# A planner's order replaced by a written one in the first third of a transformer block

## The chip, the cores and the metric

The kernel runs on one core of one Trainium2 chip, as a single program. The metric is device time in microseconds (us) from start to end; lower is better. Engines are called as the profile calls them: PE (matrix unit), PEld (its weight loads), DVE (vector), ACT (activation), POOL (GpSimd), SP (the engine that issues most transfers).

## The reference, cut to what matters

One layer over 512 latent tokens and 256 context tokens, each 1024 wide, float32.

```
h   = rmsnorm(x)   * (1 + scale)   + shift        # scale, shift = silu(c)     @ w_ada + b_ada
hc  = rmsnorm(ctx) * (1 + scale_c) + shift_c      #                c_ctx in place of c
q_c (384) | kv_c (256) | k_rope (32) | gla q,k,v (512 each) | gla gate | decay inputs (2x16) | merge gates = h @ w_in
attention, 8 heads:  q = rope(rmsnorm(q_c) @ w_uq)     k, v = rmsnorm(kv_c of h and hc) @ w_ukv, plus rope(k_rope)
                     o = softmax(q k^T / sqrt(96)) v   # 512 queries, 768 keys
gated linear attention, 4 heads, both directions, on gla q,k,v with decays from w_decay
mix = (sigmoid gates * the two branches) @ w_out;  x = x + gate1 * mix
x = x + gate2 * (gelu(conv3x3(h2 @ w_up_gate)) * (h2 @ w_up)) @ w_down;   out = rmsnorm(x) * final_g
```

## The kernel before

All matrix products keep near-float32 accuracy by splitting each operand into a high part (a cast by ACT) and a low part (a subtraction by DVE or POOL), and summing three products on PE: `mm3` (lines 124 to 128) issues high*high (line 126), high*low (127) and low*high (128). `mm` (131) is one plain product. A helper that records for every caller has one line in the profile: `sub` is line 118, `tt` 115, the ACT cast in `split` 122.

The stages that the change touches all lie in the pool `e1`:

1. **Start.** Parameter rows, the constants and the token tiles `xs[t]` (128 tokens by 1024) are loaded, the tokens' squares summed on ACT (line 366), the tokens scaled on DVE (370), and silu of the two conditioning vectors is made.
2. **Column loop**, j = 0 to 7 over the 128-column blocks of the model width. `modulation(j)` multiplies the conditioning by two 512 KB blocks of `w_ada` (32 small matmuls), copies the result (400), and turns it into the per-column shift and scale `shc`, `scc` (403, 404). `modulated(j)` transposes the tokens' block j on PE (411), applies shift and scale on ACT (413) and makes the high (416) and low (118) parts. `latents(j)` accumulates two kv and three q blocks in PSUM over j; its weights come from `load_w(j)` (320 KB into a `kT` buffer), split by ACT and POOL. `in_turn` (328 to 335) chains these loads on SP's queue, in the order in which they are written. At j = 3 `decay_weights` also issues two loads and six copies between tiles (450) on SP.
3. **Norm chain.** Squares of the kv and q latents, their sums by a one-column matmul, the factor 1/rms on ACT and DVE (170 to 179), spread over partitions by PE, and the normalised kv latents. Context tokens have a chain of their own, and q a third. `misc` projects the rope key and the decay inputs. The up-projection of q takes 128 columns a head: 64 plain, 32 rope, and the 32 rope columns again with their pairs swapped, which DVE copies out of the split weights (599, twelve copies).
4. **Attention.** For each head: `softmax(h)` makes scores for four blocks of 128 queries (six matmuls each), their maximum on DVE (694), the exponential on ACT (696), a reciprocal on DVE (697) and the scaling on POOL (698). `prep_q` makes a head's queries, whose high and low parts are both made on DVE (612, 118). `attend(h)` does six steps: four transposes of the weights (726), a high cast on ACT (729), the low part on DVE (118, tile `pl`), four matmuls with the values. `heads_out` splits a head's result (708, 710).
5. **Values of the linear attention**, `gla_v(half, t)`: 6 token tiles by 2 halves of 256 columns, 24 matmuls each; some placed between attention steps, the rest behind. Gated linear attention, merge and feed-forward follow and are not changed.

The order on each engine isn't the order of the source. The kernel is built with a planner (`schedule_with_timeline_sim`), which places each instruction by its own estimate of when it can start; `tc.issue_after` fixes single pairs. Each engine then executes its list strictly in order, so an instruction that waits holds up all behind it on its engine.

## Time and profile before

| | |
|---|---|
| median of 3 runs | 924.19 us (923.54 to 924.62) |
| the profiled execution | 922.85 us, span 921.0 us, mean granted PE clock 0.997 |
| busy PE / DVE / ACT / POOL | 890.9 / 590.5 / 400.2 / 377.4 us |
| PE matmuls | 5008 |
| loaded from memory | 97.65 MB |

The span runs from the first to the last instruction. A matmul's recorded duration includes its way through the array, so that in a steady stream the records overlap; the pace is the distance of two starts, not the duration. PE can thus be shown as busy and still not be at its pace.

### The profile page before, as it was taken

Reading aid. Unit: us, or ns where it says so; the run is one execution under the profiler, and the core shown is the slowest. Engines: PE = TensorE matmul, PEld = TensorE weight load, DVE = VectorE, ACT = ScalarE, POOL = GpSimd, SP = SyncE. Lnnn points to the kernel's source line nnn. Section 1 sums busy time; section 2 is a strip of 40 time slices with the busy share of each in tenths; the row PEclk is TensorE's granted clock in tenths of the full one; section 3 lists DMA queues with packets and bytes.
Section 4 is the critical chain, followed back from the end, with each engine's and each line's share of the span. In section 5 each row is a group of like instructions: output and inputs, shape, how many; then the busy total and the mean of one; then the engine's idle time right before and its main releaser. Section 6 shows DMA issues by size and latency. Waiting matters only on the chain.

```text
span 921.0 us, 12993 instructions
## 1 busy us (share of the span) xinstructions
PE 890.9 (97%) x5008; PEld 757.2 (82%) x5008; DVE 590.5 (64%) x984; ACT 400.2 (43%) x661; POOL 377.4 (41%) x222
## 2 busy tenths in 40 slices
PE   4989999999999999999999999999999999999996
PEld 3768788889988888888888889888888888888885
DVE  3568987867667676775674584987787876400006
ACT  3455566774445454533545232443334243422105
POOL 3354132563243434243463522354444454376403
PEclk9999999999999999999999999999999999999998
DMA  9763000042231515143981611534343433244102
GB/s 318 247 170 104 0 2 1 1 138 89 61 103 35 149 35 145 40 125 102 314 277 63 183 46 51 155 93 135 115 139 92 137 92 109 76 153 144 46 1 91
DMA packets 131229, 100.77 MB, mean 109 GB/s; under 512 B 5754, under 2 KB 122722, under 8 KB 131168
## 3 DMA queue, kind: packets, MB, share of 16 engines
q1 hardware_dynamic: 130096, 97.56, 34.9%
q0 software_dynamic: 816, 2.09, 0.7%
q8 instruction: 39, 0.64, 0.3%
q10 hardware_dynamic: 256, 0.30, 0.1%
q14 instruction: 22, 0.18, 0.1%
HBM read 97.65 MB, written 2.10 MB: 108 GB/s over the span
## 4 chain that ended last, share of the span: by engine, by line
PE 84%; DVE 4%; ACT 1%; issue 0%; ACTq 0%; DVEq 0%
PE pb L126 18%; PE pb L127 18%; PE pb L128 18%; PE p L126 7%; PE p L128 7%; PE p L127 7%; PE pb L131 4%; PE p L131 3%; PE pb L726 2%; DVE s L118 1%; DVE kT L118 1%; DVE mx L694 1%; DVE s L115 0%; PE pb L1116 0%; ACT P L696 0%
## 5 line engine op out<-in xcount | busy, mean ns | idle before, releaser
L118 POOL TENSOR_TENSOR wlo<-raw,whi 128x1024 fp32r<-128x1024 f32 (+2 forms) x113 | 257.2, 2285 | 308.2 <-ACT whi L122 281.5
L126 PE MATMUL pb<-s,whi 128*128 128x512 f32 (+1 forms) x625 | 242.4, 388 | 0.0
L127 PE MATMUL pb<-s,whi 128*128 128x512 f32 (+1 forms) x625 | 240.6, 385 | 0.0
L128 PE MATMUL pb<-s,wlo 128*128 128x512 f32 (+1 forms) x625 | 240.3, 384 | 0.0
L122 ACT CAST whi<-raw 128x1024 fp32r<-128x1024 f32 (+1 forms) x108 | 106.4, 986 | 157.3 <-issue 65.2
L128 PEld LDWEIGHTS pb<-s,wlo 128*128 128x128 f32 x625 | 117.6, 188 | 23.2
L127 PEld LDWEIGHTS pb<-s,whi 128*128 128x128 f32 x625 | 117.7, 188 | 22.7 <-issue 0.7
L126 PEld LDWEIGHTS pb<-s,whi 128*128 128x128 f32 x625 | 117.7, 188 | 22.6
L1175 DVE SCALAR_TENSOR_TENSOR ac<-pb,cwT,ac 128x441 f32<-128x441 f32 (+2 forms) x160 | 110.9, 693 | 17.9 <-ACT ac L1166 14.0
L115 DVE TENSOR_TENSOR p<-p,gt 128x512 f32<-128x512 f32 x4 | 2.8, 700 | 98.5 <-PE p L128 98.4
L126 PE MATMUL pb<-whi,s 128*128 128x256 f32 (+1 forms) x168 | 55.2, 330 | 0.0
L127 PE MATMUL pb<-wlo,s 128*128 128x256 f32 (+1 forms) x168 | 55.1, 328 | 0.0
L128 PE MATMUL pb<-whi,s 128*128 128x256 f32 (+1 forms) x168 | 55.0, 328 | 0.0
L126 PE MATMUL p<-s,s 128*128 128x512 f32 (+1 forms) x130 | 48.3, 373 | 6.7 <-DVE s L416 4.8
L698 POOL TENSOR_SCALAR P<-P,rs 128x768 f32<-128x768 f32 x32 | 29.5, 925 | 53.0 <-DVE rs L697 51.0
L127 PE MATMUL p<-s,s 128*128 128x512 f32 (+1 forms) x130 | 47.6, 366 | 0.3 <-DVE s L118 0.3
L128 PE MATMUL p<-s,s 128*128 128x512 f32 (+1 forms) x130 | 47.6, 366 | 0.0
L1177 ACT ACTIVATE ac<-ac 128x512 f32<-128x512 f32 x22 | 13.9, 633 | 76.7 <-DVE ac L1175 76.7
L126 PE MATMUL p<-s,whi 128*128 128x256 f32 (+1 forms) x130 | 43.3, 333 | 0.0
L128 PE MATMUL p<-s,wlo 128*128 128x256 f32 (+1 forms) x130 | 43.1, 332 | 0.0
L127 PE MATMUL p<-s,whi 128*128 128x256 f32 (+1 forms) x130 | 42.8, 330 | 0.0
L118 DVE TENSOR_TENSOR pl<-pb,ph 128x512 fp32r<-128x512 f32 x48 | 32.3, 683 | 12.2 <-ACT ph L729 11.9
(284 smaller groups left out, 1763.5 us busy)
## 6 DMA issues: line engine op xcount, KB each, us to landing
raw<-in_w_up_dram SPq DMA_DIRECT2D x44, 512.0 KB, 3.7
raw<-in_w_in_dram SPq DMA_DIRECT2D x32, 512.0 KB, 3.8
s<-in_w_ada_dram SPq DMA_DIRECT2D x22, 512.0 KB, 5.7
raw<-in_w_down_dram SPq DMA_DIRECT2D x22, 512.0 KB, 3.3
raw<-in_w_ada_dram SPq DMA_DIRECT2D x16, 512.0 KB, 3.8
xn<-in_w_ada_dram SPq DMA_DIRECT2D x10, 512.0 KB, 4.1
kT<-in_w_in_dram SPq DMA_DIRECT2D x8, 320.0 KB, 5.3
s<-in_x_dram SPq DMA_DIRECT2D x4, 512.0 KB, 5.4
```

The source lines that it names most:

```text
L115: return eng.tensor_tensor(out=out_, in0=a, in1=b, op=op)
L118: eng.tensor_tensor(out=out_, in0=a, in1=b, op=ALU.subtract)
L122: A.copy(hi, src)
L126: PE.matmul(o, lhsT=sh, rhs=mh, start=first, stop=False)
L127: PE.matmul(o, lhsT=sh, rhs=ml, start=False, stop=False)
L128: return PE.matmul(o, lhsT=sl, rhs=mh, start=False, stop=last)
L131: PE.matmul(o, lhsT=a, rhs=b, start=first, stop=last)
L694: V.tensor_reduce(out=mx, in_=sp[:, 0:768], op=ALU.max, axis=AX.X, negate=True)
L698: G.tensor_scalar(out=pt, in0=pt, scalar1=rs, scalar2=1.0, op0=ALU.mult, op1=ALU.mult)
L726: PE.transpose(tp[:, m * 256 + n * 128:m * 256 + (n + 1) * 128], P[2 * half + n][:, (2 * kk + m) * 128:(2 * kk + m + 1) * 128], ident)
L1175: V.scalar_tensor_tensor(out=a3[:, r0:r1, c0:c1], in0=g3[:, r0 + dy:r1 + dy, c0 + dx:c1 + dx], scalar=cw(dy, dx), in1=a3[:, r0:r1, c0:c1], ...
L1177: gelu.append(A.activation(ac, ac, AF.Gelu))
```

## The change

The first stages are written anew in the order in which they are to run. A wrapper around each engine (`Engine`) asks the planner to keep an engine's instructions in program order while its name is in `pinned`; `pinned` holds all five engines through the column loop, PE, DVE and ACT through attention, PE alone a little further (POOL until attention begins, SP until the loop ends). The parts:

- **Loads.** The constants' first 130 columns alone come first; then tokens 0 and 1, `w_ada` block 0, `w_in` block 0, tokens 2 and 3, and so on in pairs. The decay weights (two loads, six tile copies) move from j = 3 to head 2 of attention, and their subtraction from DVE to POOL. Conv weights, tables and other weights are loaded earlier in the program.
- **Column loop.** Block j+1's transposes, modulation and factors stand between block j's matmuls; context tiles are processed in j = 5 to 7, their low part on DVE instead of POOL. The last q matmuls of j = 7 are held back into the norm chain.
- **Norm chain.** The q factors and the context factors go through one chain of six columns. `w_uq`'s swapped columns are no longer made: the rope half is split twice from the raw weights (ACT cast, DVE subtraction), and the tables hold the sign and the swap. The three low parts of `w_uq` move from POOL to DVE.
- **Attention.** Software pipelining: in each of 48 steps, the next step's transposes come first, then a filler (a score block of the next head, or queries, or keys), then this step's value matmuls. The queries' high part moves from DVE to ACT, the low part (but for head 0) to POOL.
- **Values of the linear attention** take all 512 columns at once: 24 matmuls of 512 columns per token tile. Tiles 0 and 1 fill head 7's steps, tile 2 follows, tiles 3 to 5 stand behind the first `decay(0)`.

The core of the diff:

```diff
+    pinned, behind = set(), {}
+    class Engine:
+        def __init__(self, name, eng):
+            self.name, self.eng = name, eng
+        def __getattr__(self, op):
+            fn = getattr(self.eng, op)
+            def call(*args, **kw):
+                if self.name in behind:
+                    with tc.issue_after(behind[self.name].ins):
+                        return fn(*args, **kw)
+                ins = fn(*args, **kw)
+                return tc.keep_in_program_order(ins) if self.name in pinned else ins
+            return call
...
+        pinned |= {"PE", "V", "A", "G", "SY"}
...
+        SY.dma_start(out=cst[:, 0:130], in_=p["consts"][:, 0:130])
+        load_x(0)
+        load_x(1)
+        load_ada(0)
+        load_w(0)
+        load_x(2)
+        load_x(3)
+        load_ada(1)
+        load_w(1)
...
+        normalised(0, ss)
+        rows = modulation(0)
+        tp = columns(0, 0, 0, 2)
+        factors(0, rows)
+        split_latents(0)
+        modulated(0, 0, 0, 2, tp)
+        kv_latents(0, 0, 256)
+        q_latents(0, 0, 256)
+        for t in (2, 3):
+            ss = sm(1, "ssx1")
+            A.activation(junk, xs[t], AF.Square, accum_out=ss)
+            r_ = rstd_exp(ss, 1, 1.0 / D)
+            V.tensor_scalar(out=xs[t], in0=xs[t], scalar1=r_, scalar2=None, op0=ALU.mult)
...
+        for j in range(1, 8):
+            n = j + 1
+            if n < 8:
+                tp = columns(n, 0, 0, 4)
+                rows = modulation(n)
...
+            elif j == 7:
+                context(4, 8)
...
+            kv_latents(j, 0, 512)
+            if n < 8:
+                split_latents(n)
+                factors(n, rows)
+                q_latents(j, 0, 512, 0, 2)
+                modulated(n, 0, 0, 4, tp)
+                if j >= 5:
+                    context(2 * j - 10, 2 * j - 8)
+                q_latents(j, 0, 512, 2, 3)
+            extra_loads(j)
...
-            A.copy(h3[:, :, 0:96], r3)
-            sub(G, l3[:, :, 0:96], r3, f(h3[:, :, 0:96]))
-            for z in (h3, l3):
...
-                    V.tensor_copy(dst[:, :, :, s, :], src[:, :, :, 1 - s, :])
+            for (a, b, c) in ((0, 96, 0), (96, 128, 64)):
+                A.copy(h3[:, :, a:b], r3[:, :, c:c + b - a])
+                sub(V, l3[:, :, a:b], r3[:, :, c:c + b - a], f(h3[:, :, a:b]))
...
+        for k in range(2):
+            A.activation(sk[k][:, 0:512], kb_[k], AF.Square)
+        tt(V, sk[0][:, 0:512], sk[0][:, 0:512], sk[1][:, 0:512], ALU.add)
+        q_latents(7, 0, 512)
+        mwh, mwl = split_misc(mraw_[0])
+        totals(sums, sk[0], 4)
+        scaled(vk, sums[:, 0:4], 256)
+        ctx_latents(0, 4)
...
+        misc(0, 0, 3)
+        sc = EK()
+        A.activation(sc[:, 0:512], single[1], AF.Square)
+        tt(V, sc[:, 0:256], sc[:, 0:256], sc[:, 256:512], ALU.add)
+        q_latent(1)
+        q_latent(2)
+        totals(two[1][:, 512:], sq[0], 4)
+        totals(two[1][:, 516:], sc, 2)
+        misc(0, 3, 8)
+        scaled(vq[:, 0:4], two[1][:, 512:516], 384)
+        scaled(vq[:, 4:6], two[1][:, 516:518], 256)
+        rq = rstd_exp(None, 6, None, vq)
...
-            V.tensor_copy(q2[:, 0, :], X)
-            sub(V, q2[:, 1, :], X, f(q2[:, 0, :]))
+            A.copy(q2[:, 0, :], X)
+            sub(G if h else V, q2[:, 1, :], X, f(q2[:, 0, :]))
...
         for h in range(NH):
+            po = single[2 + h % 2]
+            for s in range(6):
+                next_ = turned(h + (s == 5), (s + 1) % 6) if (h, s) != (NH - 1, 5) else None
+                between(h, s)
+                weighed(h, s, po, step)
+                step = next_
+            pend = (h, po)
...
+        gla_steps = [(5, 5), (6, 0), (6, 3), (6, 3), (6, 4), (6, 4), (6, 5), (6, 5)]
+        gla_fill = [(0, 0, 2), (0, 2, 4), (0, 4, 6), (0, 6, 8), (1, 0, 4), (1, 4, 8)]
...
         dec = decay(0)
+        for t in range(3, 6):
+            gla_v(t)
+            if t > 3:
+                mod_begin(S4f)
+                mod_end()
+        pinned.clear()
+        behind["PE"] = glv[0]
```

The new functions that this calls: `turned` does a step's four transposes, the high cast on ACT and the low part on DVE (what `attend` did); `weighed` the step's four value matmuls; `between` the filler, and around it the exponentials of the score blocks still open (`exped`), their reciprocal and POOL scaling (`normed`), the keys' parts and `heads_out`.

## Rows read from the trace of the kernel before

**Rows 1.** Windows: length, busy time (count) of the engines, clock, DMA share, GB/s.

```profile
28.00:70.00 42.00, 38.72 (x313) 29.48 (x310) 25.50 (x52) 21.16 (x42) 18.82 (x20) 1.00 0.62 186
70.00:112.00 42.00, 39.28 (x231) 33.95 (x229) 39.02 (x72) 21.99 (x45) 11.73 (x9) 1.00 0.20 57
...
117.00:216.00 99.00, 96.34 (x653) 86.23 (x652) 75.21 (x125) 66.54 (x124) 43.12 (x39) 1.00 0.14 38
...
300.00:900.00 600.00, 600.00 (x2995) 505.22 (x2994) 360.02 (x564) 226.03 (x329) 252.21 (x112) 1.00 0.38 116
```

**Rows 2.** Waits of PE, first 300 us: total us, times, longest.

```profile
PE p L126 <- DVE s L416: 4.8, 3, 3.7
PE p L126 <- ACT s L122: 1.9, 1, 1.9
PE p L126 <- ACT P L696: 1.6, 2, 1.2
```

**Rows 3.** Timeline of the start: start us, us, instruction, [idle before <- releaser].

```profile
13.02 0.27 DVE L404 TENSOR_SCALAR scc<-pb,b1sc,pcol 128x2 f32<-128x2 f32 x1
...
13.25 1.06 ACT L366 ACTIVATE ph<-s 128x1024 bf16<-128x1024 f32 x1 [4.19 <-DMA s<-in_x_dram]
...
15.49 0.55 ACT L413 ACTIVATE P<-pb,shc,scc 128x256 f32<-128x256 f32 x1
...
16.51 0.55 PE L126 MATMUL p<-s,s 128*128 128x256 f32 x1 [3.67 <-DVE s L416]
```

**Rows 4.** Timeline: two starts of 256-column matmuls at 18 us.

```profile
18.06 0.41 PE L127 MATMUL p<-s,s 128*128 128x256 f32 x1
18.27 0.41 PE L128 MATMUL p<-s,s 128*128 128x256 f32 x1
```

**Rows 5.** Timeline: full pace, 512 columns, then 256 columns (`gla_v`).

```profile
151.70 0.39 PE L126 MATMUL pb<-s,whi 128*128 128x512 f32 x1
151.93 0.39 PE L127 MATMUL pb<-s,whi 128*128 128x512 f32 x1
...
222.09 0.28 PE L128 MATMUL pb<-whi,s 128*128 128x256 f32 x1
222.21 0.28 PE L126 MATMUL pb<-whi,s 128*128 128x256 f32 x1
```

**Rows 6.** Timeline of SP's queue, ACT and PE around the weight loads, 42 to 59 us.

```profile
42.49 7.40 SPq L450 DMA_DIRECT2D s<-s  x6
49.98 0.53 SPq L335 DMA_DIRECT2D kT<-in_w_in_dram  x1
...
53.20 0.41 ACT L122 CAST s<-kT 128x256 fp32r<-128x256 f32 x1 [1.72 <-DMA kT<-in_w_in_dram]
...
58.51 0.65 PE L131 MATMUL pb<-raw,s 128*32 128x128 f32 x16
```

**Rows 7.** Timeline of POOL and DVE in the norm chain.

```profile
76.88 3.66 POOL L118 TENSOR_TENSOR wlo<-raw,whi 128x768 fp32r<-128x768 f32 x2
...
76.93 3.70 DVE L599 CAST whi<-whi 128x128 fp32r<-128x128 f32 x2
...
82.01 0.35 DVE L599 CAST whi<-whi 128x128 fp32r<-128x128 f32 x2
```

**Rows 8.** DVE and ACT groups by form, 112 to 216 us: count | busy us, mean ns | idle before.

```profile
L118 DVE TENSOR_TENSOR pl<-pb,ph 128x512 fp32r<-128x512 f32 x43 | 28.9, 683 | 10.0 <-ACT ph L729 9.7
...
L118 DVE TENSOR_TENSOR s<-X,s 128x512 fp32r<-128x512 f32 x5 | 4.1, 811 | 0.2
L612 DVE CAST s<-X 128x512 fp32r<-128x512 f32 x5 | 3.5, 708 | 0.1
...
L729 ACT CAST ph<-pb 128x512 fp32r<-128x512 f32 x44 | 25.7, 587 | 20.1 <-PE pb L726 13.2 <-PE pb L131 3.0 <-PE p L128 2.6
```

**Rows 9.** Timeline: the same wait of PE in heads two apart.

```profile
145.66 0.38 PE L131 MATMUL pb<-pl,s 128*128 128x256 f32 x1 [0.34 <-DVE pl L118]
...
173.59 0.38 PE L131 MATMUL pb<-pl,s 128*128 128x256 f32 x1 [0.34 <-DVE pl L118]
```

More of the change, by code (lines that the diff above doesn't have):

```diff
@@ new lines, in load_wq, with load_wkv, split_latents @@
+        def load_wq(k):
+            wq_raw.append(EK())
+            SY.dma_start(out=wq_raw[k], in_=w_uq[:, k, :])
+        def load_wkv(k):
+            wkv_raw.append(raw_tile())
+            SY.dma_start(out=wkv_raw[k], in_=w_ukv[:, k, :])
+        kvw = [[S4([128, 4, 256]) for _ in range(2)] for _ in range(2)]
+        wpair = []
+        def split_latents(j):
+            r = wraw[j]
+            if j % 2 == 0:
+                wpair[:] = whl()
+            wj[j] = [w[:, j % 2 * 384:j % 2 * 384 + 384] for w in wpair]
+            for (h_, l_), w in (([kvw[j // 4][i][:, j % 4, :] for i in range(2)], r[:, 384:640]), (wj[j], r[:, 0:384])):
+                split(h_, l_, w)
@@ new lines, in factors, with columns @@
+        def factors(j, rows):
+            mm(mp[:, 0:2], rows[:, 0:128], sel)
+            mm(mp[:, 2:4], rows[:, 128:256], sel)
+            V.tensor_scalar(out=shc[:, j, :], in0=mp[:, 0:2], scalar1=col("b_ada", j), scalar2=None, op0=ALU.add)
+            V.tensor_scalar(out=scc[:, j, :], in0=mp[:, 2:4], scalar1=b1sc[:, j:j + 1], scalar2=col("norm1_g", j),
+                            op0=ALU.add, op1=ALU.mult)
+        tps = [0]
+        def columns(j, ctx_, t0, n):
+            tps[0] += not ctx_
+            tp = (mp if j < 6 else single[2])[:, j % 2 * 256:j % 2 * 256 + 256] if ctx_ else single[1 + tps[0] % 2]
+            for t in range(n):
+                PE.transpose(tp[:, t * 128:(t + 1) * 128], xs[4 * ctx_ + t0 + t][:, j * 128:(j + 1) * 128], ident)
+            return tp
@@ new lines, in block_kernel @@
+        rows = modulation(0)
[10 more added lines that the diff above has]
+            V.tensor_scalar(out=xs[t], in0=xs[t], scalar1=r_, scalar2=None, op0=ALU.mult)
+        rows = modulation(1)
+        tp = columns(0, 0, 2, 2)
@@ new lines, in weighed, with gla_v_load @@
+        def weighed(h, s, po, x2_):
+            half, kk = divmod(s, 3)
+            vs = slice(h * 128, (h + 1) * 128)
+            for m in range(2):
+                kt = 2 * kk + m
+                for x in x2_:
+                    mm(po[:, half * 256:(half + 1) * 256], VV[kt][:, vs], x[:, m * 256:(m + 1) * 256],
+                       kt == 0 and x is x2_[0], kt == 5 and x is x2_[1])
+        glav, wv, gps, glv, m0 = [], [], {}, [None], []
+        graw = []
+        def gla_v_load(i):
+            graw.append(S4f())
+            SY.dma_start(out=k3(graw[i], 2, 512), in_=w_in[:, 2 * i:2 * i + 2, CGV:CGV + 512])
@@ new lines, in between @@
+        def between(h, s):
+            n = ((0, 1, 2, None, 3, None), (None, 0, 1, 2, 3, None))[h % 2][s]
+            exped()
+            if h + 2 < NH and (h % 2, s) == (0, 5):
+                key_parts(1)
+            if h + 1 < NH and n is not None:
+                scores(h + 1, n)
+            if h + 2 < NH and s == (5, 0)[h % 2]:
+                prep_q(h + 2, wide()[:, 0:512] if h % 2 else single[3])
+            if h > 0 and s == h % 2:
+                heads_out(*pend)
+            normed()
+            if h + 2 < NH and (h % 2, s) == (0, 3):
+                keys(h // 2 + 1)
+                key_parts(0)
+            if h == 2:
+                next(dw, None)
+            if h == 5 and 1 <= s <= 4:
+                gla_v_load(s - 1)
+            for k in range(KT):
+                if (h, s) == gla_steps[k]:
+                    gla_v_split(k)
+            if (h, s) == (1, 2):
+                pinned.add("G")
+                misc_parts()
+                pinned.discard("G")
+            if h == 0 and s < 2:
+                values(4 + s, single[3])
+                values_out(4 + s, single[3])
+            if (h, s) == (6, 5):
+                begun.append(mp_tile())
+                m0.append(mod_steps(3072, begun[0], raw_tile))
+                next(m0[0])
+                behind["SY"] = load[0]
+            if h == 7:
+                gla_v(*gla_fill[s])
+                for _ in range(2 if s else 0):
+                    next(m0[0], None)
```

724 lines of the change are left out of this document (378 added, 346 removed).

## The prediction, made before the run

> **What bounds the kernel now.** I read the windows first, to see where PE is not busy: PE is the engine whose work adds up to the span, so only time that it loses can be won. From 300 to 900 us it is busy for all 600 us [rows 1]; nothing is to be had there, and the change does not touch it. In the stretches that are rewritten it lost 3.28 us of 42 (28 to 70 us), 2.72 of 42 (70 to 112) and 2.66 of 99 (117 to 216) [rows 1], and at the start 3.67 us in one wait [rows 2, 3]. Then I read the list of PE's waits, which says what ended each: the high part of the tokens, a weight cast, the exponential [rows 2]. These are all cases of PE's list asking for something that another engine had not been told to make early enough. Last I read the pace, the distance of two starts: 0.23 us for 512 columns, 0.12 us for 256 [rows 5]. A record lasts 0.28 to 0.39 us, so a wait shorter than some 0.16 us is not shown as idle, and one that is shown cost about 0.16 us more than the idle time says. The losses above are therefore lower bounds.
>
> The amount of PE work hardly changes: the same products, transposes and sums are made. So the question is how much of the lost time the new order gets back, and which new waits it puts in its place.
>
> **The start.** The scale for the first block is there at 13.02 + 0.27 = 13.29 us, but ACT applies it only at 15.49: its list had two squares of later tokens in front, the first of which itself waited for its transfer [rows 3]. The new order puts the first block ahead of these squares: 15.49 - 13.4 = 2.1 us. This holds if the first latent weights are there; their load is moved ahead of two token loads of 512 KB each, so it lands earlier than before, when the first matmul at 16.51 waited for the tokens' high part and not for weights [rows 3]. Two ends: nothing, if the weights or the factors are late by as much, and 2.1 us. In this stretch 256 columns take 0.21 us [rows 4], about 1.2 GHz worth of columns, and 0.12 us later [rows 5], the 2.4 GHz level, though the window's granted clock reads 1.00. If the rise to full pace stays where it is on the time axis, work that is done earlier is done at half pace and half of the 2.1 us is lost again; if it moves with the work, none is. I take 1.9. The Trainium skill (TensorE: Matmul & The Clock Gate, Part 1, The HAM clock gate) says that the array starts throttled and that sustained activity releases it, which would move the rise with the work and give 2.1; the rows agree that the rise came after the steady stretch from 16.51 had begun, and show no more.
>
> **The loads.** The six tile copies of the decay weights held SP's queue from 42.49 to 49.9 us; the next `w_in` block was issued behind them at 49.98, its cast ran at 53.20 and PE waited 1.9 us for it [rows 2, 6]. The copies go to head 2, where SP's list is short. The rest of the 3.28 us in this window comes from waits of the same loop (line 416, 4.8 us in three waits, of which 3.7 were the start) [rows 2]. In the new loop PE has per block 6 + 9 matmuls of 512 columns, two sets of 16 small ones at 0.65 [rows 6] and 8 of at most 128 columns: 15 * 0.23 + 1.3 + 8 * 0.12 = 5.7 us. A block of loads is 1.37 MB; the window moved 186 GB/s at a DMA share of 0.62 [rows 1], so some 300 GB/s when full, 4.6 us. From the factors to the low part the chain is two small DVE steps (0.5), ACT (at most twice the 0.55 of [rows 3]), a cast and a subtraction on DVE (0.71 and 0.68 [rows 8]) and hand-overs, at most 3.3 us; PE has three q blocks, the next transposes and the next modulation in front of its use, 9 * 0.23 + 0.5 + 1.3 = 3.9 us. So the loop should run without waits. Ends 1.0 and 3.28 + 4 * 0.16 = 3.9; I take 3.6.
>
> **The norm chain.** Here DVE is as full as PE: 39.02 of 42 us [rows 1]. Part of that was waste: two copies of `w_uq` columns took 3.70 us beside two POOL subtractions of 3.66, and 0.35 us alone [rows 7]. All twelve copies go. But DVE takes over the `w_uq` subtractions (three of 768 columns and three of 256) and the low parts of the eight context blocks: by columns, at 0.68 for 512 [rows 8], 3 * 1.05 + 11 * 0.4 = 7.5 us, about as much as goes. Counting the new list from the last kv latents to the first scores: 20 operations of 512 columns at 0.70, 5 of 768 at 1.05, 7 of 256 at 0.4, and some 4 us of others, together 26 us; on PE 69 matmuls of 512 columns, 78 of 256 and 20 of fewer: 69 * 0.23 + 98 * 0.12 = 27.6 us. Walking both lists I find two places where PE stands. First the kv sums: from block 7's factors PE has q blocks, context transposes, kv and the last q latents, 2.1 + 1.3 + 1.4 + 2.1 = 6.9 us, while DVE has 0.5, a wait of 1.1 for ACT, block 7's two parts 1.4, six context blocks 4.5, a `w_uq` split 1.5 and the addition 0.7, 9.7 us: a wait of 2.8. Then the q sums, whose PSUM bank is read until the second q latent is split: PE has 24 * 0.12 + 9 * 0.23 = 5.0 us, DVE 1.5 + 1.4 + 0.7 + 1.4 + 1.4 + 0.4 + 0.7 = 7.5 with 0.4 us of lead: 2.1. Together 4.9 us, against 2.72 [rows 1], 1.6 for the exponentials just behind [rows 2] and six restarts at 0.16, 5.3 us, that were lost. Ends: a loss of 1.5, if these waits are a third longer (6.8 us), and a gain of 3.3, if only the second occurs; I take 0.4.
>
> **Attention.** The same wait recurs at 145.66 and at 173.59 [rows 9], so two heads take 27.9 us. PE's work in two heads at full pace: 48 transposes and 48 value matmuls at 0.12, 8 score blocks at 3 * 0.23 + 3 * 0.12, queries 18 * 0.23, keys 6 * 0.23 + 6 * 0.12: 26.2 us. So 1.75 us are lost per pair of heads, 6.1 us in seven heads. The new order puts between a step's transposes and their use a filler, four matmuls, four transposes and mostly another filler: 1.03 + 0.47 + 0.44, that is 1.9 us, and 2.9 with the second, against a chain of ACT 0.59, DVE 0.68 [rows 8] and hand-overs, 1.6 us. What is queued in front on those engines is an exponential or a maximum of 768 columns, about 1 us each by columns. DVE loses 0.71 + 0.81 us per head [rows 8] to ACT and POOL, which makes its work in two heads some 3 us less, 75.21 / 99 * 27.9 - 3.0 = 18.2 us [rows 1] against PE's 26.2. Some 0.1 us at each change between transposes and products stays. Ends 0 and 6.1; I take 4.6, some 0.4 us per pair of heads remaining.
>
> **Values of the linear attention.** 288 matmuls of 256 columns at 0.12 become 144 of 512 at 0.23 [rows 5]: 34.6 - 33.1 = 1.5 us; ends 0 and 1.5, I take 1.3. Moving three tiles behind `decay(0)` gives PE work during that chain; I count nothing, since PE was nearly full there.
>
> **Costed at nothing.** ACT's new casts, the tables, the earlier conv loads on POOL's queue and the wrapper: ACT is busy 66.5 us of 99 and POOL 43 [rows 1], and PE's work covers them; if that cover went, the ACT share would cost up to 0.6 us per head.
>
> **Sum.** 1.9 + 3.6 + 0.4 + 4.6 + 1.3 = 11.8 us; 922.85 - 11.8 = 911.05 in the profiled execution, which lies 1.34 us under the median of the runs: 912.4 there, which I take.
>
> **Rivals.**
> 1. *DVE becomes the bound of the norm chain* (0.15). Speaks for it: 26 against 27.6 us, and the stretching in [rows 7]: four subtractions of `w_ukv` on POOL, each up to 1.8 us, run beside it. If DVE stands for all of them, 7.2 us, its list is 33.2 us, PE waits another 5.6 us, and the total gain falls to 6.2: 918. It decides once POOL holds DVE for over 1.6 us, the margin. Against: most DVE operations there read PSUM. The Trainium skill (SBUF — State Buffer, Who interferes with whom) says that DVE and GpSimd share a port pair that one of them holds for a whole instruction, also against DVE operations with two inputs in SBUF; [rows 7] agree, the copies lasting as long as the POOL work beside them.
> 2. *The waits only move* (0.06): PE loses elsewhere what it gains, 921 to 926. For: PE is at 93% and above in each window already [rows 1]. Against: the waits have causes by name, which the new order removes.
> 3. *In order, one late result holds a whole engine* (0.10). Nothing can fill in any more. The place is the step in attention: if each of 48 steps waits for its low part as at 173.59, 0.34 us [rows 9] and 0.2 for restarting, that is 26 us in place of the 6.1 lost now, less the 7.2 won elsewhere: 924 + 13 = 937; it decides from some 0.28 us per step on, the restart counted. Against: the cover of 1.9 to 2.9 us for a chain of 1.6.
> 4. *Nearly all is won* (0.04), the upper ends together, 2.1 + 3.9 + 3.3 + 6.1 + 1.5 = 16.9 us, 907, and losses too short to show: 903 to 907.
>
> My forecast has 0.65. The range holds it with rivals 1 and 4 and leaves out most of 2 and 3: 903 to 921. The least that a measurement of this kernel can tell is about 0.2%, 1.8 us. Faster: 0.65 + 0.15 + 0.04 and a little of rival 2, 0.85; same 0.05; slower 0.10.
>
> **What would show it.** Start: the first latent matmul near 14.4 us instead of 16.5. Loads: no PE wait over 0.3 us between 26 and 60, and the last q latents ending near 63. Norm chain: PE waits of 2 to 5 us in all, on the kv and the q sums, with DVE above 90% busy. Attention: a pair of heads in about 26.7 us. The span from 300 us on should be the same work shifted. I am wrong if the loop waits for loads, if the first matmul does not move, or if steps in attention show a regular wait.

## The result, and the profile after

The changed kernel takes 918.12 us (median of 5 runs, 915.61 to 919.78), the kernel before, timed beside it, 923.54 (922.32 to 924.62): a ratio of 0.994 [0.9916, 0.9964]. That is 5.4 us faster where 11.8 were forecast; the range held it, the gain was less than half of the forecast. The profiled execution took 919.78 us, 3.07 less than the 922.85 of before. It is the slowest of the five; why the five differ by 4 us is not settled (last section).

The page of the changed kernel gives the busy time and count of each engine. All operations now go through one wrapper, so that nearly every line is L87 or L88, and groups are told apart by their tiles:

```profile
PE 889.5 (97%) x4864; PEld 751.7 (82%) x4864; DVE 574.8 (63%) x963; ACT 399.9 (44%) x663; POOL 382.0 (42%) x231
```

The windows of the changed kernel (length, busy time and count of PE, PEld, DVE, ACT, POOL, granted clock, DMA share, GB/s) answer to [rows 1]:

```profile
26.00:63.00 37.00, 36.49 (x324) 29.15 (x322) 21.96 (x55) 16.56 (x34) 11.33 (x13) 1.00 0.79 247
63.00:99.00 36.00, 33.61 (x197) 29.37 (x198) 27.02 (x50) 20.30 (x39) 6.79 (x5) 0.95 0.00 0
76.00:80.00 4.00, 4.00 (x16) 3.29 (x16) 2.02 (x7) 1.44 (x4) 0.00 (x0) 0.62 0.00 0
106.00:134.00 28.00, 26.81 (x175) 23.83 (x174) 20.15 (x35) 17.54 (x33) 12.00 (x12) 1.00 0.01 3
162.00:190.00 28.00, 26.76 (x178) 23.78 (x176) 20.30 (x34) 19.20 (x38) 12.38 (x13) 1.00 0.25 76
200.00:207.00 7.00, 5.51 (x24) 4.25 (x23) 3.08 (x5) 4.50 (x9) 7.00 (x7) 0.76 0.23 72
300.00:900.00 600.00, 600.00 (x2992) 504.97 (x2991) 359.15 (x569) 226.07 (x331) 251.23 (x112) 1.00 0.38 114
```

The column loop (first row) is now full: 0.51 us idle in 37. From 300 us on nothing changed. The loss sits in the norm chain, in each 28 us of attention (1.2 us idle), and in the end of the attention loop; and in two places PE is shown busy at a mean granted clock of 0.62 and 0.76, so partly at the lower of its two levels (1.2 and 2.4 GHz). PE's timeline of the changed kernel, at the places where it stands (start, us, instruction, idle before and who ended it), answers to [rows 3] and [rows 9]:

```profile
14.21 0.58 PE L88 MATMUL p<-s,s 128*128 128x256 f32 x1 [1.48 <-DVE s L88]
...
62.58 0.39 PE L88 MATMUL pb<-s,wlo 128*128 128x512 f32 x1
...
75.20 1.50 PE L88 MATMUL p<-ones,kT 128*128 128x1 f32 x12 [1.25 <-DVE s L88]
76.56 3.84 PE L88 MATMUL pb<-s,s 128*128 128x512 f32 x9
...
121.25 0.72 PE L88 MATMUL p<-s,whi 128*128 128x512 f32 x2 [0.40 <-DVE kT L88]
...
129.25 1.32 PE L88 MATMUL p<-kT,s 128*128 128x512 f32 x6 [0.79 <-ACT P L88]
...
195.15 1.32 PE L88 MATMUL p<-kT,s 128*128 128x512 f32 x6 [0.98 <-ACT P L88]
...
203.19 0.76 PE L88 MATMUL p<-whi,s 128*128 128x512 f32 x1 [0.89 <-ACT raw L88]
203.75 0.63 PE L88 MATMUL p<-wlo,s 128*128 128x512 f32 x1
```

The first latent product starts at 14.21 instead of 16.51, the last q latents end near 63. Behind the 1.25 us wait nine matmuls of 512 columns last 3.84 us, some 0.43 each, against 0.23 at full pace [rows 5]. In attention the wait for the low part [rows 9] is gone, but two others have come, 0.40 and 0.79 us, and they come again at 149.17 and 157.19 and at 177.11 and 185.12: a pair of heads takes 27.9 us (129.25 to 157.19), as before. The waits at 195.15 and 203.19, with 0.26 and 0.34 us between them (200.52 and 201.25), belong to the end of attention.

Where the 0.79 us wait comes from is read in four engines' timelines of the changed kernel, here in order of time:

```profile
123.05 1.29 POOL L88 TENSOR_TENSOR s<-X,s 128x512 fp32r<-128x512 f32 x1
124.37 0.69 DVE L88 TENSOR_TENSOR X<-p,qtab 128x512 f32<-128x512 f32 x1 [0.46 <-POOL s L88]
125.09 0.62 ACT L88 CAST s<-X 128x512 fp32r<-128x512 f32 x1 [1.91 <-DVE X L88]
125.79 1.29 POOL L88 TENSOR_TENSOR s<-X,s 128x512 fp32r<-128x512 f32 x1 [1.46 <-ACT s L88]
127.11 0.58 ACT L88 COPY X<-pb 64x512 f32<-64x512 f32 x1 [0.44 <-POOL s L88]
128.20 0.91 ACT L88 ACTIVATE P<-p,mx 128x768 f32<-128x768 f32 x1
```

X is a single buffer: it holds a head's rotated queries and then, in `heads_out`, the rest of a head's result. GpSimd reads it for the queries' low part, 1.29 us where VectorE needed 0.81 [rows 8], so both the next head's X and `heads_out`'s copy stand until GpSimd is through; ScalarE, in order, stands with its copy; the exponential behind it is late; and it alone frees the PSUM buffer that the next scores want.

### The profile page after: what moved, and what is told of

Read it like the earlier page. It is cut to its first block, busy times and chain, and to the rows that moved or that the text cites. A ratio compares the mean times of both kernels' runs of the same rounds, so it can differ in the third digit from the quotient of the medians.

```text
span 918.0 us, 12643 instructions
## 1 busy us (share of the span) xinstructions
PE 889.5 (97%) x4864; PEld 751.7 (82%) x4864; DVE 574.8 (63%) x963; ACT 399.9 (44%) x663; POOL 382.0 (42%) x231
## 4 chain that ended last, share of the span: by engine, by line
PE 86%; DVE 5%; ACT 4%; issue 2%; POOL 1%; DMA 1%; POOLq 0%; DVEq 0%; ACTq 0%
PE pb L88 45%; PE p L88 22%; PE pb L87 14%; PE p L87 6%; DVE s L88 1%; DVE kT L88 1%; POOL s L88 1%; ACT ph L88 1%; DMA raw<-in_w_ada_dram 1%; ACT P L88 1%; DVE mx L88 1%; ACT s L88 1%; ACT raw L88 1%; DVE X L88 1%; ACT kT L88 1%
## 5 line engine op out<-in xcount | busy, mean ns | idle before, releaser
L88 POOL TENSOR_TENSOR wlo<-raw,whi 128x1024 fp32r<-128x1024 f32 (+1 forms) x106 | 240.9, 2279 | 338.8 <-ACT whi L88 310.3
L88 PE MATMUL pb<-s,whi 128*128 128x512 f32 (+1 forms) x906 | 272.3, 383 | 0.0
L88 PEld LDWEIGHTS pb<-s,whi 128*128 128x128 f32 x906 | 167.6, 188 | 32.2
L88 ACT CAST whi<-raw 128x1024 fp32r<-128x1024 f32 (+1 forms) x106 | 103.3, 975 | 178.0 <-issue 77.3
L88 PE MATMUL pb<-s,wlo 128*128 128x512 f32 (+1 forms) x453 | 172.9, 382 | 0.0
L88 DVE SCALAR_TENSOR_TENSOR ac<-pb,cwT,ac 128x441 f32<-128x441 f32 (+2 forms) x160 | 111.0, 694 | 19.3 <-ACT ac L88 15.4
L87 PE MATMUL pb<-s,whi 128*128 128x512 f32 x320 | 101.8, 396 | 0.0
L88 PEld LDWEIGHTS pb<-s,wlo 128*128 128x128 f32 x453 | 85.3, 188 | 16.5
L88 PE MATMUL p<-s,s 128*128 128x512 f32 (+1 forms) x392 | 83.5, 369 | 1.7 <-DVE s L88 1.7
L88 PEld LDWEIGHTS p<-s,s 128*128 128x128 f32 x392 | 66.4, 191 | 15.0 <-DVE s L88 2.3
L88 PE MATMUL p<-whi,s 128*128 128x512 f32 x208 | 69.9, 397 | 1.0 <-ACT raw L88 0.9
L87 PEld LDWEIGHTS pb<-s,whi 128*128 128x128 f32 x320 | 58.9, 188 | 12.4 <-issue 0.7
L88 DVE TENSOR_TENSOR p<-p,gt 128x512 f32<-128x512 f32 x4 | 2.8, 699 | 98.5 <-PE p L88 98.4
L87 PE MATMUL pb<-s,wlo 128*128 128x512 f32 x160 | 62.8, 392 | 0.0
L88 PE MATMUL pb<-whi,s 128*128 128x512 f32 x176 | 57.5, 390 | 0.0
L88 PEld LDWEIGHTS p<-whi,s 128*128 128x128 f32 x208 | 39.5, 190 | 9.6 <-ACT raw L88 1.1
L88 DVE TENSOR_TENSOR pl<-pb,ph 128x512 fp32r<-128x512 f32 x48 | 33.0, 687 | 20.0 <-ACT ph L88 19.9
L88 PE MATMUL p<-kT,s 128*128 128x512 f32 (+1 forms) x192 | 41.2, 351 | 3.6 <-ACT P L88 3.6
L88 PE MATMUL pb<-s,s 128*32 128x128 f32 (+2 forms) x322 | 43.6, 335 | 1.1 <-DMA s<-in_w_ada_dram 1.1
L88 PE MATMUL p<-wlo,s 128*128 128x512 f32 x104 | 41.0, 394 | 0.0
L88 ACT ACTIVATE ac<-ac 128x512 f32<-128x512 f32 x22 | 13.9, 632 | 60.8 <-DVE ac L88 60.8
L88 PE MATMUL p<-s,whi 128*128 128x256 f32 (+1 forms) x156 | 39.1, 342 | 1.3 <-DVE kT L88 1.2
```

The lines of the kernel that those rows point to most:

```text
L87: return fn(*args, **kw)
L88: ins = fn(*args, **kw)
```

## The experiments

Fourteen kernels, each timed beside the kernel before; a time is a median, with its ratio to the kernel before and the interval of that ratio. The changed kernel (0.994 [0.9916, 0.9964]) is the base unless the text says otherwise; none leaves work out. The first four each change one thing, and by their times alone none of them stands apart from the changed kernel, since the intervals overlap: what they show is in their traces.

**The low part of the queries back on VectorE.**

```diff
-        sub(G if h else V, q2[:, 1, :], X, f(q2[:, 0, :]))
+        sub(V, q2[:, 1, :], X, f(q2[:, 0, :]))
```

> The changed kernel, with the low part of each head's queries back on DVE (the change had moved it to POOL). Theory A: attention gained nothing because the single X buffer is held until POOL has subtracted, so that heads_out's second ACT copy, the exponential behind it and then a score block of PE wait (0.79 us of PE in each pair of heads, 0.16 for restarting). Then this wait goes in all pairs, two heads take some 27.0 us instead of 27.9, and the whole is some 2.5 to 3.5 us faster than the changed kernel (918.1). Rival B: the loss is in the switches between transposes and products, not in waits: two heads stay at 27.9 us. Rival C: DVE is short of time in attention: the wait turns up elsewhere and two heads get longer.

916.88 us, 0.9926 [0.9905, 0.9946]. The 0.79 us wait is gone in all three pairs, the 0.40 stays, and a pair takes 27.3 us, 0.6 less, where I expected 0.9 less. The mechanism is shown, its size was overestimated (PE's timeline; the wait recurs at 177.25):

```profile
122.69 0.73 PE L88 MATMUL p<-s,whi 128*128 128x512 f32 x2 [0.40 <-DVE kT L88]
...
149.99 0.74 PE L88 MATMUL p<-s,whi 128*128 128x512 f32 x2 [0.40 <-DVE kT L88]
```

**The rest of a head's result in another buffer.**

```diff
-        rest = tl(e1, [128, 512], F32, "X", 1)
+        rest = tl(e1, [128, 512], F32, "pl", 2)
```

> The changed kernel, with heads_out's second copy in a buffer of the tile pl, as before the change, instead of X; the queries' low part stays on POOL. Theory A (the shared X buffer makes ACT wait for POOL): the copy's wait of 0.44 us goes and the PE wait of 0.79 us falls to 0.3 or less, 1.5 to 3 us in all. Rival: ACT's own list (cast, two copies, cast, exponential) is what is too long, whichever buffer: the wait stays above 0.6 us.

917.83, 0.9936 [0.9915, 0.9956]. The wait falls to 0.47, 0.46 and 0.51 us, a pair takes 27.8: the shared buffer holds ScalarE for part of the wait, but less than expected (0.3 or less was to be left). VectorE's write of the next head's X still waits 0.46 us for GpSimd here, at 122.00, and the rest of PE's wait goes only when the operation leaves GpSimd, as in the experiment above.

**The keys' second half taken first.**

```diff
-            exped()
             if h + 2 < NH and (h % 2, s) == (0, 5):
                 key_parts(1)
+            exped()
```

> The changed kernel with one swap: in the fifth step of each even head the second half of the keys is taken off its PSUM buffer before the pending exponentials, not after them. Theory A (the 0.40 us wait of each pair, where the query product waits for the buffer that the keys' casts still read, is set by ScalarE's place for that cast): the wait falls below 0.1 us in three pairs, a pair of heads takes 27.5 to 27.6 us where it takes 27.93, and the kernel gains 0.8 to 1.4 us: about 917.0. Rival: the exponential that now comes later lets the next scores product wait as long (scores wait for a buffer that the exponential frees): a new wait of 0.3 us or more on ScalarE's P after this step, the pair unchanged within 0.1 us, no gain.

916.42, 0.993 [0.9917, 0.9942]; the 0.40 us wait is gone, the other 0.57 to 0.61, a pair 27.0 us. The step was worth more than its own wait, 0.9 us a pair.

```profile
128.70 1.31 PE L88 MATMUL p<-kT,s 128*128 128x512 f32 x6 [0.57 <-ACT P L88]
...
155.75 1.32 PE L88 MATMUL p<-kT,s 128*128 128x512 f32 x6 [0.61 <-ACT P L88]
```

**Five tiles of the miscellaneous product ahead of the q sums, instead of three.**

```diff
-        misc(0, 0, 3)
+        misc(0, 0, 5)
...
-        misc(0, 3, 8)
+        misc(0, 5, 8)
```

> The changed kernel, with five instead of three of the eight misc blocks of latents ahead of the q and context sums, 1.4 us of PE work more in front of the place where PE waits 1.25 us for the second q latent. Theory A: the wait goes, and with it the stretch of 3 to 4 us at half pace that follows it (granted clock 0.81 and 0.50 from 75.3 to 80): 1.2 + 1.2 to 1.7, that is 2 to 3 us faster than the changed kernel. Rival: the half pace has another cause than this wait and stays, 1.2 us or less; or the factor chain then ends late and PE waits at the spread instead, nothing.

915.65, 0.9923 [0.9903, 0.9944]. In the profiled run the 1.25 us wait is gone, and so is every stretch at a lower clock (0.998 over the whole run), the one at the end of attention too, though the waits there are unchanged; four of its six runs have a mean of 0.995 or 0.996. A pair is unchanged at 27.9. Attention's first score block starts 2.6 us earlier than in the changed kernel (first line: this kernel; second: the changed one), so that the wait of 1.25 us and what followed it cost about twice the wait:

```profile
96.18 2.36 PE L88 MATMUL p<-kT,s 128*128 128x512 f32 x12 [0.21 <-ACT P L88]
```

```profile
98.78 2.38 PE L88 MATMUL p<-kT,s 128*128 128x512 f32 x12 [0.23 <-ACT P L88]
```

**The gla values' loads and splits a head earlier.**

```diff
-            if h == 5 and 1 <= s <= 4:
-                gla_v_load(s - 1)
+            if h == 4 and s <= 3:
+                gla_v_load(s)
...
-        gla_steps = [(5, 5), (6, 0), (6, 3), (6, 3), (6, 4), (6, 4), (6, 5), (6, 5)]
+        gla_steps = [(4, 4), (4, 5), (5, 1), (5, 2), (5, 3), (5, 4), (5, 5), (6, 0)]
```

> The changed kernel, with the weights of the linear attention's values loaded in head 4 and split from the end of head 4 on, instead of in head 6, where PE has 9.6 us of work and ACT some 12.7. Theory A: ACT's eight casts are what PE waits for at the end of head 6 and the start of head 7 (0.98, 0.26, 0.34, 0.89 us) and the half pace from 203 to 206.5 us follows from that: 2.5 to 4 us faster than the changed kernel, granted clock 1.00 there. Rival: heads 4 and 5 are as short of ACT time, the waits only move there: within 1 us of the changed kernel.

919.41, 0.996 [0.9944, 0.9975]: no gain. In PE's timeline the recurring wait of 0.79 us has grown to 1.33 in one pair, one of 1.48 us is new, and of the four waits at the end 0.98 and 0.89 stay:

```profile
186.29 1.32 PE L88 MATMUL p<-kT,s 128*128 128x512 f32 x6 [1.33 <-ACT P L88]
...
191.63 0.55 PE L88 MATMUL pb<-cst,P 128*128 128x128 f32 x3 [1.48 <-POOL P L88]
...
198.03 1.32 PE L88 MATMUL p<-kT,s 128*128 128x512 f32 x6 [0.98 <-ACT P L88]
...
205.31 0.50 PE L88 MATMUL p<-whi,s 128*128 128x512 f32 x1 [0.89 <-ACT raw L88]
```

The new wait is for GpSimd, where two subtractions of the splits (1.29 us at 187.27, 1.28 us at 189.41) stand between the scalings of the score blocks. Before the 0.98 us wait one split stands in the first step of head 6, here as in the changed kernel. The 0.89 us wait is the same with no split left near it: head 7's first gla product takes the PSUM buffer of the last score block, and waits for that block's maximum (from 203.23) and exponential (from 204.27). So that wait is not the splits' doing.

**Attention without the kept order.**

```diff
-        pinned.discard("G")
+        pinned.clear()
         pend = None
```

(and no kept order for GpSimd in one step.)

> The changed kernel with the attention loop's kept order taken away on all engines: the start, the column loop and the norm chain stay as written, and inside the loop over heads the scheduler again orders each engine's instructions by its own costs. Theory A (the written order in attention is worth about nothing, what it wins in the wait for pl it gives back in the 0.40 and 0.79 us waits): within 1.5 us of the changed kernel, a pair of heads 27.8 to 28.0 us, with the 0.31 us waits for pl back and the 0.79 us wait for P gone or smaller. Rival 1 (the written order wins what was forecast and something else in the loop took it, the query's low part on GpSimd): slower than the changed kernel by 2 to 4 us, pair 28.5 us or more. Rival 2 (the written order itself costs): faster by 2 us or more, pair 27.3 or less.

931.9 us, 1.0092 [1.0073, 1.011]. The reading of attention was right, that of the time wrong. PE's timeline of this kernel:

```profile
156.09 0.50 PE L88 MATMUL p<-kT,s 128*128 128x512 f32 x1 [0.51 <-ACT P L88]
...
184.04 0.50 PE L88 MATMUL p<-kT,s 128*128 128x512 f32 x1 [0.29 <-ACT P L88]
...
259.69 1.02 PE L88 MATMUL pb<-ones,mp 128*128 128x1 f32 x4 [7.94 <-DVE mp L88]
```

Two heads take 27.95 us: free or written, the order is worth the same here, with the queries' low part still on GpSimd. (A free order without that was run only as the kernel before, where a pair takes 27.9.) What is lost comes behind the loop, where VectorE's list, placed anew, mixes the modulation rows with the decay's operations and brings them 7.94 us late.

**Three of these together** (the query's low part, the keys first, five tiles).

> The changed kernel with three edits together: the query's low part on VectorE again, the keys' second half taken before the pending exponentials, and five instead of three tiles of the miscellaneous product ahead of the two sums. If the three costs are separate (theory A: 0.65 us per pair, 0.35 us per pair, and 1.25 us with the half pace that follows it), the gains add: 916.9 is what the first alone gave, 915.7 the third alone, the second is expected at 0.8 to 1.4, so 912.5 to 914.5, a pair of heads at 26.9 to 27.0 us. Rival (they share one bound, VectorE's or ScalarE's own list in attention): no more than the better of the single ones, 915 to 917, pair at 27.2 or more.

911.87 us, 0.9889 [0.9873, 0.9904], 6.3 us below the changed kernel, where the three alone were 1.2, 1.7 and 2.5 below it: by the medians the gains add, and this interval is clear of the changed kernel's. VectorE's maxima of the same score block stand a pair apart, 26.4 us (the next at 176.37); and the window of attention of this kernel has no idle time:

```profile
123.59 0.95 DVE L88 TENSOR_REDUCE mx<-p 128x1 f32<-128x768 f32 x1
...
150.03 0.95 DVE L88 TENSOR_REDUCE mx<-p 128x1 f32<-128x768 f32 x1
```

```profile
106.00:134.00 28.00, 28.00 (x187) 25.41 (x186) 21.96 (x38) 20.05 (x39) 11.79 (x13) 1.00 0.01 4
```

**The same with the gla splits in steps without an exponential.**

```diff
-        gla_steps = [(5, 5), (6, 0), (6, 3), (6, 3), (6, 4), (6, 4), (6, 5), (6, 5)]
+        gla_steps = [(4, 4), (5, 0), (5, 0), (6, 4), (6, 4), (6, 5), (7, 0), (7, 1)]
```

(with the loads in head 4 as above.)

> The version with the three edits (911.9 us), with the gla values' loads in the fifth head instead of the sixth and their eight splits put into steps without an exponential: one in the fifth step of head 4, two in the first step of head 5, two in the fifth and one in the last step of head 6, and one in each of the first two steps of head 7. Theory A (ScalarE's casts for these splits, two to a step ahead of the copies and exponentials of heads 6 and 7, make the waits of 1.00, 0.26, 0.34 and 0.89 us at 188 to 197): these fall to 0.5 us in sum or less, and the kernel gains 1.5 to 2.5 us: 909.4 to 910.4. Rival (the same casts hold the copies wherever they stand, as when they were put into heads 4 and 5 in every step): new waits of the same sum in heads 4 and 5 or 7, 911 to 913.

910.9 us, 0.9862 [0.984, 0.9884]. Of the four waits at the end 0.98, 0.26 and 0.34 are gone, 0.89 us remains, and 0.80 has come at 179.86: of 2.5 us of waits 1.0 us of time was won by the medians, and the two intervals overlap, so that the gain is not shown.

**The first context products ahead of the kv sums.**

```diff
+        ctx_latents(0, 2)
         totals(sums, sk[0], 4)
         scaled(vk, sums[:, 0:4], 256)
-        ctx_latents(0, 4)
+        ctx_latents(2, 6)
...
-        ctx_latents(4, 8)
+        ctx_latents(6, 8)
```

> The same, and the products of the first two context tiles put ahead of the sums over the latents' squares, with two tiles fewer behind the spread. Theory A (the sums' wait of 0.93 us for VectorE's total of the squares is only a matter of what stands ahead of it on TensorE): the wait at 64 goes, no new one of 0.3 us or more comes before 80, and no half pace: 0.7 to 1.0 us better than without it, 908.5 to 909.7. Rival 1 (the chain from the sums to the scaled copies is then later and VectorE ends the stage as before): the gain comes back as a wait at the spread or at the later sums, no difference. Rival 2 (a new short wait lets the clock fall): a window of granted clock under 0.9 between 63 and 99 and 1 to 3 us lost.

911.67 us, 0.9873 [0.9854, 0.9893]: no gain. The first wait is gone; the one at the q sums is back, with the clock behind it (timeline and window of this kernel):

```profile
74.84 1.50 PE L88 MATMUL p<-ones,kT 128*128 128x1 f32 x12 [1.28 <-DVE s L88]
```

```profile
76.00:80.00 4.00, 4.00 (x14) 3.17 (x14) 2.02 (x7) 1.44 (x4) 0.00 (x0) 0.57 0.00 0
```

**And seven tiles ahead of the q sums.**

```diff
-        misc(0, 0, 5)
+        misc(0, 0, 7)
...
-        misc(0, 5, 8)
+        misc(0, 7, 8)
```

> The version with the gla splits spaced and the context products ahead of the first sums (911.7 us), with seven instead of five tiles of the miscellaneous product ahead of the two later sums. Theory A (VectorE's own list is the bound of this stage, so that a later place for the sums only moves the wait): the 1.28 us wait at 75 goes, a wait of 0.8 to 1.5 us on VectorE's or ScalarE's factors comes at the spread behind it, 911 to 912. Rival (what stood ahead of the sums on TensorE was the cause): no wait of 0.3 us or more and no half pace between 60 and 99, 909.0 to 910.2.

909.64 us (908.96 to 909.89), 0.9856 [0.9838, 0.9875], the best of all. Neither theory as stated: one wait of 0.59 us stays at the spread, and the clock holds. What stood ahead of the sums was most of it; VectorE's and ScalarE's chain of factors is the rest.

```profile
77.41 0.82 PE L88 MATMUL pb<-cst,rr 128*128 128x128 f32 x5 [0.59 <-DVE rr L88]
```

**The kernel before with the decay loads moved alone.**

```diff
-                decay_weights()
...
+            if h == 2:
+                decay_weights()
```

> The kernel before with one part of the change alone: the decay weights' loads and splits are taken out of the column loop and begun in the third head of attention, nothing else moved. Theory A (SP's queue, held by these loads until their splits are done, is why the later weights come late): the 1.9 us wait of TensorE in the column loop falls below 0.4 us and the stretch up to the last latents is 1.5 to 2.5 us shorter; the kernel 921.0 to 922.0, against 923.5. Rival (the loads come earlier and the loop then waits for ScalarE's and VectorE's own lists): the wait is replaced by others of the same sum, 923 to 924, no change.

925.4 us, 1.003 [1.0018, 1.0041]: slower by 0.3%, where 1.5 to 2.5 us of gain, or none, was expected. The 1.9 us wait is gone; the time is lost in the norm chain, in a wait more than twice as long as that of before and with the clock behind it (PE's timeline, first line of the kernel before, second of this one; window):

```profile
83.12 1.13 PE L131 MATMUL pb<-cst,rr 128*128 128x128 f32 x8 [0.91 <-DVE rr L179]
```

```profile
80.86 1.13 PE L131 MATMUL pb<-cst,rr 128*128 128x128 f32 x8 [2.18 <-DVE rr L179]
```

```profile
83.00:87.00 4.00, 4.00 (x20) 4.00 (x21) 3.61 (x12) 2.14 (x7) 0.00 (x0) 0.50 0.08 25
```

**The kernel before with the start moved alone.**

```diff
         for half in range(2):
             modulated(0, 0, 2 * half, 2)
+            if half == 0:
+                normalise(2, 2)
```

(and taken out ahead of the loop.)

> The kernel before with one part of the change alone: the norm factors of the second pair of token tiles are written behind the first half of the first modulated tile, not ahead of it. Theory A (those factors on VectorE and ScalarE are what the first latent product waits for): it starts near 14.4 where it started at 16.5, and the kernel gains 1.0 to 2.3 us, 921.5 to 922.5. Rival (the gain is given back further on, in the column loop's own waits for loads and in the norm chain, as the earlier decay loads' was): the first product at 14.4, the last latents within 0.5 us of before, no change, 923 to 924.

923.07 us, 0.9999 [0.9985, 1.0013]; the first product at 17.14. This tells nothing of the start: ScalarE still has both squares ahead of the first block, as its timeline shows. The planner put the moved lines back.

```profile
13.78 1.06 ACT L366 ACTIVATE ph<-s 128x1024 bf16<-128x1024 f32 x1 [4.27 <-DMA s<-in_x_dram]
...
15.06 1.06 ACT L366 ACTIVATE ph<-s 128x1024 bf16<-128x1024 f32 x1
...
16.12 0.55 ACT L413 ACTIVATE P<-pb,shc,scc 128x256 f32<-128x256 f32 x1
```

**The changed kernel with the start undone alone**: the squares of tokens 2 and 3 ahead of the first block.

```diff
+        s23 = [sm(1, "ssx1") for _ in range(2)]
+        for t in (2, 3):
+            A.activation(junk, xs[t], AF.Square, accum_out=s23[t - 2])
         modulated(0, 0, 0, 2, tp)
```

> The changed kernel with its start undone alone: the two squares of the third and fourth token tile stand ahead of the first modulated tile on ScalarE again. In the kernel before, the same edit of the start could not be made by moving lines, because the scheduler put the instructions back where they had been. Theory A (ScalarE in order, held by these squares, is what the first latent product waits for, and TensorE is busy from there to 63, so nothing takes the delay up): the first latent product at 16.3 to 16.8 where it stood at 14.2, the last latents end 1.8 to 2.4 us later, the kernel 919.8 to 920.6. Rival (a delay at the start is taken up by the waits of the loop and the norm chain, as the loads alone in the kernel before won 2.3 us and lost them again by 92): the last latents within 0.5 us, 918 to 918.6.

919.51 us (917.5 to 921.64), 0.9969 [0.9957, 0.9981]. The first product comes at 15.61 and not at 16.3 or later, as the tokens landed sooner than in the kernel before; of these 1.4 us 0.95 are left at the last matmul of the q latents (63.53 against 62.58). The 0.45 between is the full pace, which came sooner in that run: the first two sets of sixteen small matmuls behind the first product last 0.65 and 0.62 us where those of the changed kernel last 1.08 and 0.68. So the delay is not taken up, but it is smaller than I expected, and by its time this kernel is not told apart from the changed one.

```profile
15.61 0.58 PE L88 MATMUL p<-s,s 128*128 128x256 f32 x1 [3.23 <-DVE s L88]
```

**The changed kernel with the decay loads back in the loop.**

```diff
             elif j == 3:
+                for _ in decay_weights():
+                    pass
                 load_ada(6)
...
-        dw = decay_weights()
+        dw = iter(())
```

> The changed kernel with the decay weights' loads put back alone: loads, splits and stores at tile 3 of the column loop, ahead of the loads of tiles 6 and 7, as in the kernel before, but with the splits on GpSimd. Theory A (SP's queue holds until the splits are done and the weights of tile 6 come late): a wait of TensorE of 1 to 2 us between 45 and 60, the kernel 919.3 to 920.3. Rival (GpSimd has nothing else to do there, the splits come at once, and the queue is held for less than the weights' lead): no wait of 0.3 us or more in the column loop, 918 to 918.6, and the 1.9 us of before came from VectorE's place for these splits.

920.38 us, 0.9979 [0.9962, 0.9996], at the edge of the changed kernel's interval; the profiled run took 923.23. The six copies hold SP's queue for 4.94 us (7.40 in the kernel before [rows 6], where VectorE and not GpSimd made the splits), the weights come late, and PE waits for transfers; the last matmul of the q latents starts at 65.97, 3.4 us later.

```profile
38.67 4.94 SPq L88 DMA_DIRECT2D s<-s  x6
```

```profile
47.83 0.32 PE L88 MATMUL pb<-s,s 128*32 128x128 f32 x4 [0.68 <-DMA s<-in_w_ada_dram]
...
49.31 0.32 PE L88 MATMUL pb<-raw,s 128*32 128x128 f32 x4 [0.84 <-DMA raw<-in_w_ada_dram]
...
56.14 0.32 PE L88 MATMUL pb<-raw,s 128*32 128x128 f32 x4 [0.59 <-DMA raw<-in_w_ada_dram]
```

## Why the prediction was half right

All of this is in the time of the profiled executions, where 3.07 us were won.

**Start, forecast 1.9.** Right by the trace: the first product came 2.3 us earlier. It stands between 13.72 and 14.83 in all twelve kernels with the new start, at 16.51, 16.64 and 17.14 in the kernel before and its two variants. The full pace moved with the work: a set of sixteen small matmuls takes 1.08 us for the last time at 17.95 instead of 20.32, and 0.68 at 18.81 where 0.65 was first seen at 22.39 (two lines of the kernel before, then two of the changed one).

```profile
20.32 1.08 PE L131 MATMUL pb<-s,s 128*32 128x128 f32 x16
...
22.39 0.65 PE L131 MATMUL pb<-raw,s 128*32 128x128 f32 x16
```

```profile
17.95 1.08 PE L88 MATMUL pb<-s,s 128*32 128x128 f32 x16
18.81 0.68 PE L88 MATMUL pb<-raw,s 128*32 128x128 f32 x16
```

That agrees with what the Trainium skill says (TensorE: Matmul & The Clock Gate, Part 1, The HAM clock gate), that activity releases the array's throttle. How far it moved is in part the luck of two profiles: in the two variants of the kernel before the set lasts 0.64 us already at 20.45 and 20.63, and in the one with the keys taken first it still lasts 1.08 at 18.59. Undone alone the start gave back 1.4 us; the rest I put down to the order of the loads, since in that run the tokens came 1.1 us sooner (12.18 against 13.25 [rows 3]).

**Loads, forecast 3.6.** Right: 0.51 us idle where 3.28 were lost [rows 1], 2.8 us, and two or three restarts. The holding of SP's queue is shown in both directions, by the experiment that takes the copies out of the kernel before and the one that puts them back into the changed kernel. That the gain reaches the end is no matter of course: alone in the kernel before it was lost again in the norm chain.

**Norm chain, forecast 0.4.** What the new chain loses was sized rightly as a sum, and its parts were not. The waits on the kv and q sums were 0.93 and 1.25 us where I had 2.8 and 2.1, and VectorE was busy 75% (27.02 of 36), not above 90%; with the two short waits behind (0.23 each) and four restarts at 0.16 PE lost 3.3 us. The clock took 1.8 more, 36 us at 0.95: together 5.1 where 4.9 were forecast. What the old chain lost was too high, though. My 5.3 us added the exponentials' 1.6 to the window's 2.72, but the longer of these two waits lies for 1.04 us inside that window (kernel before):

```profile
112.20 0.50 PE L126 MATMUL p<-kT,s 128*128 128x512 f32 x1 [1.24 <-ACT P L696]
```

With five waits, not six, the old chain lost 4.1 us, so the forecast should have been -0.8, and by this count 1.0 us was lost. Rival 1, VectorE as the bound, did not come.

**Attention, forecast 4.6: the step that failed.** I credited VectorE with the work that it loses to ScalarE and GpSimd, set against the cover only "an exponential or a maximum" as what is queued in front, and costed ScalarE's new casts at nothing. I did not ask who waits for the operation once it is on a slower engine. The low part of the queries is on no critical path by itself; the single buffer that it reads is, through a copy and an exponential on ScalarE, and so the time lost per pair was lost again, at other places: 0.40 and 0.79 us and two restarts, 1.5 of the 1.75. Putting that operation back and taking the keys before the exponentials makes a pair 26.4 us, below the 26.7 that I forecast. So the cover of 1.9 us and more for the chain of 1.6 was counted rightly, and two details of the placing ate all of it. This was rival 3's mechanism (a late result holds an engine that runs in order), but in two of twelve steps of a pair and not in all.

**The end of attention, not costed.** The place of the gla values' eight splits was in the prediction at most as part of "ACT's new casts", at nothing. Heads 6 and 7 have waits of 0.98, 0.26, 0.34 and 0.89 us, four restarts at 0.16, and 7 us at a clock of 0.76, together 4.8 us, 3.1 more than a pair of before lost. The first three waits are the splits', one split in the first step of head 6 and two to a step behind it on ScalarE: in the version that differs from the three edits only in the place of the splits these waits are gone. The 0.89 us stayed wherever the splits stood, and belongs to the first gla product, written directly behind the last score block whose PSUM buffer it takes. The lower clock, 1.7 of the 4.8, followed these four waits in three profiles of the eight that have them.

**Sum.** 2.3 + 2.8 - 1.0 + 0 - 3.1 = 1.0 of the 3.07. The other 2.1 are the wider gla products (forecast 1.3, not measured alone), the loop's restarts and what I did not see; the account by waits does not close better than that. With the placing mended the change gives 909.64 us, 12.8 below the kernel before timed beside it (922.45): the forecast's 11.8 was there to be had.

## What to carry to other kernels

When an operation moves to a slower engine to relieve a full one, follow its input buffer and not only its result: who writes that buffer next, on which engine, and what stands behind that instruction. An engine kept in written order does exactly what is written, so every small insertion (a split, a cast) belongs in a step whose engine has room, and a filler must be as long as the chain that it covers at that place, not as the average. In a kernel whose order a planner sets, moving lines is no experiment until the order on the engines has been looked at.

## What the runs showed of the hardware that was not expected

The clock fell after waits of PE that were short. Each of the six kernels whose q sums waited 1.25 to 1.28 us ran partly at the lower level just behind (mean granted clock 0.57 to 0.77 over four microseconds). The wait at the kv sums, 0.91 to 0.93 us, was followed by it in four kernels of the eleven that had it, and waits of 1.92 and 2.01 us at the same spot in the kernel before and in its variant with the start moved were followed by 1.00 over 53 to 57 us in the one and by 0.67 in the other. The length of the wait alone does not decide: in attention, waits of 1.33 and 1.48 us (the splits a head earlier) were followed by 1.00 from 184 to 200 us. What decides was not settled.

Whether this is why the five runs of the changed kernel spread over 4.2 us is not shown. Their mean clocks are not in the order of their times (915.61 at 0.995, 918.12 at 0.996, 919.78 at 0.994), and the version with context products first, with its stretch at 0.57, spreads over only 0.4 us. In the kernel before the two mostly go together: of 23 runs ten at 0.998 have a median of 921.99, eight at 0.996 one of 923.29, and two at 0.993 took 925.91 and 926.85.
